# First chunk of a head without its zero-state products, and per-token columns by transposes

## The chip, the cores and the metric

The kernel runs on one core of one Trainium2 chip. The metric is device time in microseconds, from the start to the end of one execution. All matrices live in memory as fp32; most products run as three fp32r products of a high and a low part.

## What is computed

One layer of a streaming encoder, for a new stream of 2048 tokens (the prompt) and 64 tokens of a running stream (the sample), model width 1024. Cut to what matters here:

```python
h = rmsnorm(x, norm1_w)
proj = h @ w_in                 # q,k,v (4 heads x 128 each), z, a, b (4 each), pooling input
qkv = silu(causal_conv4(qkv));  q, k l2-normalised
g = -exp(a_log) * softplus(a + dt_bias);  beta = sigmoid(b)
G = cumsum(g) within a chunk    # per token and head
# per chunk and head, with state S (128 x 128):
v_new = u - w @ S               # u = T (beta v),  w = T (beta exp(G) k)
o     = (q exp(G)) @ S + (q k^T * gamma) @ v_new
S     = S * exp(G_last) + (k exp(G_last - G))^T @ v_new
x = x + concat(rmsnorm(o) * silu(z), pool(u_pool)) @ w_out
x = x + (silu(rmsnorm(x) @ w_gate) * (rmsnorm(x) @ w_up)) @ w_down
```

The prompt's state S starts at zero; the sample's comes as an input. Outputs are the tokens and the states after the last token.

## The kernel before

The work has two phases. In phase one the tokens go through in four blocks: block 0 has 512 prompt tokens and the 64 of the sample, the others 512 each. A block's normed input is multiplied by 21 weight tiles of `w_in` (names `pp`, `project`): tile 0 gives the columns a and b, then come q, k, v and z of each of four heads, then four pooling tiles. Phase two is the feed-forward part, with Strassen-like products, and isn't touched.

All instructions are first noted and then put in order by a list scheduler written in the kernel (`Machine`, its `issue`): it keeps a planned time for each engine and for each tile's buffers, and takes on each engine the operation with the lowest rank of those ready. Rank is the place in the program, less a boost: `HOT_ROWS` for the function `rows`, 400 for evictions. A tile gets a buffer of its tag when its first operation is ready. For each tag but the three common matmul banks (`psmm`, tag `mm`) only the head of the queue is looked at, so a tag's tiles get buffers in the order in which the program made them. `issue` starts all engines from that order; each engine runs its list in order.

PSUM has eight banks here: three of tag `mm`, one each of `k` and `o`, and three of tags `b0` to `b2`, given by `bank(i, name)`, each with one buffer. The chains of a head (`Front`) use `b0` to `b2` in turn; before any head is ready these banks serve the start of block 0:

```python
pab = project(B, 0)            # block 0: its halves go to banks o and k
rows(B, pab)
...                            # then head_project -> project(B, 1 + 4*h + i)
out = [[bank(("ok", (1, 2))[m][i], f"pp{m}_{i}") if B.j == 0 and m < 2 else psmm(...)
```

So in block 0 the first half of tile 1 (`pp1_0`, tokens 0 to 287) goes to bank 1 and the second half (`pp1_1`) to bank 2. Within a half, block 0 runs 24 products for each tile (8 parts of the depth times 3); in the other blocks the tokens are not halved.

A weight tile arrives as two raw parts (`wrp` in the profile), each is cast (ScalarE) and its rest subtracted (VectorE) into a split part (`wsp`, four buffers, so two tiles' worth), and in block 0 the split part is also stored to memory (`wnd<-wsp`) for the later blocks. A split part's buffer is free when its products are done and its store has landed.

`rows` makes the per-token rows from a and b: it adds the norm's factor, takes softplus, multiplies by the coefficient (`Rt`, rows 0 to 3 g, rows 32 to 35 the log of beta), sums g within each chunk of 128 tokens, and puts G_last - G in rows 64 to 67. Then it turns them into per-token columns with a product with a 0/1 matrix `sel12` for each chunk (12 columns, tile `pc`), and takes the exponential into `EC`; for the sample, the same into `ECs`. In block 0 `pc` lies in bank 0, behind two sums of the norm and one small product.

`Head.prompt` runs the recurrence over a head's four chunks of 128 tokens: product of k with S, subtraction (`rhs`), product with the inverse `X`, scaling (`vn`), state update product, and the two products of the output `po`. The state `Sp` is zeroed at the start.

Of the kernel before, what the change touches and what calls it, by code (L numbers as in the profile page):

```python
# [11 lines left out]
F32 = mybir.dt.float32  # L12
F32R = mybir.dt.float32r
AF = mybir.ActivationFunctionType
ALU = mybir.AluOpType
# [3 lines left out]
P = 128  # L19
# [5 lines left out]
C = 128  # L25
# [12 lines left out]
SO = PB[0] + 3  # L38
# [331 lines left out]
def hybrid_kernel(ctx, tc, a, o):  # L370
    nc = machine = Machine(tc.nc)
    act = nc.scalar.activation
    tt = nc.vector.tensor_tensor
    ts = nc.vector.tensor_scalar
# [7 lines left out]
    def mm(out, lhsT, rhs, start, stop, **kw):  # L382
        nc.tensor.matmul(out, lhsT, rhs, start=start, stop=stop, **kw)
        n = 1
        for d in out.shape[1:]:
            n *= d
        cost(n, rhs.dtype)
# [527 lines left out]
    B = Block(0)  # L915
# [13 lines left out]
    pcnt = names["pcnt"].rearrange("p (g t) -> p g t", t=16)  # L929
    poolw = names["poolw"].rearrange("p (g t) -> p g t", t=P)  # L930
    sgn, dtb, alog = names["sgn"], names["dtb"][:64], names["alog"][:64]
    sel12 = names["sel12"]
    hist = names["sconv"].rearrange("p (m i t) -> p m i t", i=2, t=3)
    phist = names["spool"].rearrange("p (m i t) -> p m i t", i=2, t=HP)
    Ss = names["sdelta"].rearrange("p (h v) -> p h v", v=P)
# [32 lines left out]
        nc.gpsimd.tensor_copy(*((t, x) if keep else (x, t)))  # L968

    Sp = cp1.tile([P, NH, P], F32, tag="Sp", name="Sp")  # L970
    nc.vector.memset(Sp, 0.0)

    def bc(t, nch, n):
        return t.unsqueeze(1).to_broadcast([t.shape[0], nch, n])
# [164 lines left out]
    class Head:  # L1139
# [37 lines left out]
        def prompt(self):  # L1177
            tag, h, B = self.tag, self.h, self.B
            S = Sp[:, h, :]
            po = bank("o", f"po_{tag}")  # L1180
            qsq = self.squares(512)
            for f in self.f:
                yield lambda: f.done
                for c in range(2):
                    pk = bank("k", f"pk{c}_{f.tag}")
                    mm(pk[:, :P], f.chunk(1, c), S, start=True, stop=True)
                    rhs = gp.tile([P, P], F32, tag="rhs", name=f"rhs{c}_{f.tag}", bufs=2)
                    stt(rhs, pk[:, :P], f.e(0)[:, c : c + 1], f.vtk[:, c, :], ALU.mult, ALU.subtract)
                    yield LAT_D
                    mm(pk[:, P : 2 * P], f.X[:, c], rhs, start=True, stop=True)  # L1190
                    vn = gp.tile([P, P], F32, tag="vn", name=f"vn{c}_{f.tag}", bufs=2)
                    act(vn, pk[:, P : 2 * P], AF.Copy, scale=f.kn[:, 2, c : c + 1])
                    yield LAT_D
                    osl = slice((f.c0 + c) * C, (f.c0 + c + 1) * C)
                    mm(pk[:, 2 * P : 3 * P], f.ktl[:, c, :], vn, start=True, stop=True)
                    mm(po[:, osl], S, f.Qd[:, c, :], start=True, stop=False)
                    mm(po[:, osl], vn, f.QKG[:, c], start=False, stop=True)
                    stt(S, S, f.EL[:, c], pk[:, 2 * P : 3 * P], ALU.mult, ALU.add)
                    yield LAT_D
                f.used = True  # L1200
            osq = yield from self.norm(512, po, qsq)
            if B.kept:
                nc.sync.dma_start(out=od[h], in_=osq)
                return
            yield lambda: B.o is not None
            split(B.o[h], slice(0, 512), osq)
# [36 lines left out]
    def rows(B, pab):  # L1243

        j, YW, nch = B.j, B.YW, B.nch
        Ghl = B.Ghl = gp.tile([P, SO + P], F32R, tag="Ghl", name=f"Ghl{j}", bufs=2)
        EC = B.EC = gp.tile([P, 4, 16], F32, tag="EC", name=f"EC{j}", bufs=2)
        xr = gp.tile([64, YX], F32, tag="w2", name=f"xr{j}", bufs=2)
        er = gp.tile([64, YX], F32, tag="w2", name=f"er{j}", bufs=2)
        if B.dec:  # L1250
            nc.gpsimd.memset(xr, 0.0)
        for i, b, n, dst in B.segs:
            x, lo = xr[:, dst : dst + n], B.subs[i][0] + b
            act(x, pab[i][:64, b : b + n], AF.Identity, scale=sgn[:64], bias=0.0 if j == 0 else dtb)
            stt(x, pab[i][64:, b : b + n], sgn[64:], x, ALU.mult, ALU.add)
            if j == 0:
                tt(x, x, B.r[:64, lo : lo + n], ALU.mult)
                ts(x, x, dtb, None, ALU.add)
        act(er[:, :YW], xr[:, :YW], AF.Abs)
        act(er[:, :YW], er[:, :YW], AF.Exp, scale=-1.0)  # L1260
        act(er[:, :YW], er[:, :YW], AF.Ln, bias=onec[:64])
        stt(er[:, :YW], xr[:, :YW], 0.0, er[:, :YW], ALU.max, ALU.add)
        Rt = gp.tile([P, SO + P], F32, tag="w2", name=f"Rt{j}", bufs=2)
        nc.gpsimd.memset(Rt[64:], 0.0)
        nc.gpsimd.memset(Ghl[64:].bitcast(F32), 0.0)
        ts(Rt[:64, :YW], er[:, :YW], coef, None, ALU.mult)
        chunks = [(c * C, C) for c in range(nch)] + ([(SO, DEC)] if B.dec else [])
        for lo, n in chunks:
            nc.vector.tensor_tensor_scan(Rt[0:4, lo : lo + n], ones[0:4, :n], Rt[0:4, lo : lo + n], 0.0,
                                         ALU.mult, ALU.add)  # L1270
        for c, (lo, n) in enumerate(chunks):
            ts(Rt[64:68, lo : lo + n], Rt[0:4, lo : lo + n], Rt[0:4, lo + n - 1 : lo + n], -1.0,
               ALU.subtract, ALU.mult)
        if B.dec:
            nc.vector.tensor_copy(Rt[:, SO + DEC : SO + P], Rt[:, SO : SO + DEC])
            chunks[-1] = (SO, P)
        pc = psg(f"pc{j}") if j else bank(0, "pc0")
        for c, (lo, n) in enumerate(chunks):
            mm(pc[:n, c * 12 : c * 12 + 12], Rt[:, lo : lo + n], sel12, start=True, stop=True)
        pc3 = pc[:, : 12 * nch].rearrange("p (c t) -> p c t", t=12)  # L1280
        act(EC[:, :nch, :12], pc3, AF.Exp)
        act(EC[:, :nch, 12:], pc3[:, :, :4], AF.Copy, scale=-1.0)
        if B.dec:

            ECs = B.ECs = cp1.tile([P, 4, 2], F32, tag="ECs", name="ECs")
            for i in range(2):
                t = slice(i * DEC, (i + 1) * DEC)
                of = pc[t, 12 * nch : 12 * nch + 12].rearrange("p (t c i) -> p t c i", t=3, i=2)[:, :, :, i]
                act(ECs[t, :3], of, AF.Exp)
                act(ECs[t, 3], of[:, 0], AF.Copy, scale=-1.0)  # L1290
            YW += DEC
        nc.vector.tensor_copy(Ghl[0:32, :YW], Rt[0:32, :YW])
        tt(Ghl[32:64, :YW], Rt[0:32, :YW], Ghl[0:32, :YW].bitcast(F32), ALU.subtract)
# [467 lines left out]
    for op in order:  # L1761
# [23 lines left out]
        else:  # L1785
# [56 lines left out]
WAIT_STAT = 8.46  # L1842

CONSTS = (("ident", 128), ("convw", 48), ("onw", 1), ("psc", 4), ("pcnt", 64), ("poolw", 512), ("sgn", 1),
          ("dtb", 1), ("alog", 1), ("sel12", 12), ("sel", 4), ("sconv", 72), ("spool", 120), ("sdelta", 512))


def _layout(inp):
# [56 lines left out]
        lm[:, l, :] /= WSCALE  # L1905
    lm[:, 7, :] = np.where(i[None] >= i[:, None], 0.0, -1e30)
    r["lmask"] = lm
    z = np.zeros((P, 12), f32)
    for t in range(3):
        for h in range(4):  # L1910
            z[32 * t + h, 4 * t + h] = 1.0
    c["sel12"] = z
    z = np.zeros((P, 4), f32)
    for h in range(4):
        z[h, h] = 1.0
# [40 lines left out]
```

## Time and profile before

| | before |
|---|---|
| median of three runs | 2296.41 us |
| lowest and highest run | 2295.73, 2298.98 us |
| span of the profiled execution | 2295.8 us |
| TensorE busy | 2271.8 us (99%) |
| VectorE busy | 1711.3 us (75%) |
| ScalarE busy | 1342.1 us (58%) |
| GpSimd busy | 833.4 us (36%) |

The span goes from the first to the last instruction of one profiled execution; the page gives no other time of that execution, and the median of the runs is 0.6 us above it. In the profile PE is TensorE and PEld its weight loads, DVE VectorE, ACT ScalarE, POOL GpSimd, SPq the queue of SyncE that issues DMAs. Every instruction has line 285, the helper that issues the planned order, so work is told apart by its tiles: `out<-in`. An fp32 product is two records of TensorE, an fp32r product or a transpose one. A row of the timeline gives its start, the time from its first to its last end, engine, operation, tiles, count, and in brackets an idle time before it with what ended it. A row by tile gives count, shortest, median and longest duration in ns, and the first and last start.

### The profile page before, as it was taken

What the parts mean: (1) busy time and instruction counts of PE and PEld (TensorE: products, weight loads), DVE (VectorE), ACT (ScalarE), POOL (GpSimd) and SP (SyncE); (2) the same over time, 40 slices, a digit from 0 to 9 for tenths busy, and PEclk for the clock granted to TensorE, in tenths of its full rate; (3) what the DMA queues carried; (4) which work ended last, traced back from release to release, by engine and by line L of the source; (5) the groups of instructions that cost most, each with busy time, mean ns of one, the idle gap of its engine ahead of it and who ended that gap; (6) DMA issues with size and microseconds to landing.
All of it is one profiled execution on the core that took longest, in us unless ns stands there. A gap on an engine that the chain in (4) does not pass through costs nothing.

```text
span 2295.8 us, 41549 instructions
## 1 busy us (share of the span) xinstructions
PE 2271.8 (99%) x14518; PEld 2132.1 (93%) x14518; DVE 1711.3 (75%) x3129; ACT 1342.1 (58%) x3039; POOL 833.4 (36%) x893
## 2 busy tenths in 40 slices
PE   8999999999999999999999999999999999999998
PEld 8898898888787888999999999999999999999998
DVE  8989876685678896788888786866667768666576
ACT  6986866684769864565446366554334574353344
POOL 3425342453247450565434236622111453010112
PEclk9999999999999999999999999999999999999999
DMA  8755586578476767866776578778765776666653
GB/s 295 263 182 193 199 294 234 191 238 277 159 245 232 212 212 254 304 247 247 272 260 238 185 264 292 248 266 302 234 198 199 263 271 230 209 216 224 210 195 103
DMA packets 256514, 536.96 MB, mean 234 GB/s; under 512 B 30000, under 2 KB 94000, under 8 KB 256304
## 3 DMA queue, kind: packets, MB, share of 16 engines
q1 hardware_dynamic: 255728, 533.58, 69.3%
q8 instruction: 114, 1.87, 0.3%
q14 instruction: 96, 0.79, 0.1%
q10 hardware_dynamic: 576, 0.72, 0.1%
HBM read 403.62 MB, written 130.58 MB: 233 GB/s over the span
## 4 chain that ended last, share of the span: by engine, by line
PE 88%; DVE 5%; DMA 3%; ACT 2%; issue 1%; POOL 1%; SPq 0%; DVEq 0%; POOLq 0%; ACTq 0%
PE px L285 21%; PE pp L285 17%; PE pz L285 13%; PE py L285 10%; PE dx L285 8%; PE dy L285 4%; PE d L285 3%; PE dz L285 2%; PE pk_p L285 2%; PE pt_p L285 2%; PE gr_p L285 1%; DVE y L285 1%; PE py_p L285 1%; DVE h L285 1%; DMA hpd<-xt 1%
## 5 line engine op out<-in xcount | busy, mean ns | idle before, releaser
L285 PE MATMUL pp<-h,wsp 128*128 128x512 f32 (+1 forms) x2480 | 547.9, 364 | 10.0 <-DVE wsp L285 10.0
L285 PEld LDWEIGHTS pp<-h,wsp 128*128 128x128 f32 x2480 | 401.4, 189 | 58.2 <-ACT wsp L285 9.2
L285 ACT CAST ws<-wr 128x512 fp32r<-128x512 f32 x198 | 122.1, 618 | 166.7 <-PE dx L285 55.2
L285 DVE TENSOR_TENSOR ws<-wr,ws 128x512 fp32r<-128x512 f32 x198 | 173.4, 879 | 30.9 <-ACT ws L285 27.1
L285 POOL TENSOR_TENSOR q<-hr,hr 128x352 f32<-128x352 f32 x52 | 58.0, 1116 | 369.6 <-DVE hr L285 366.8
L285 ACT CAST wsd<-wrd 128x512 fp32r<-128x512 f32 (+1 forms) x120 | 62.6, 526 | 174.8 <-PE dx L285 66.8
L285 DVE TENSOR_TENSOR y<-y,dx 128x352 f32<-128x352 f32 x240 | 121.8, 517 | 57.0 <-PE dx L285 56.0
L285 PE MATMUL pz<-op,wsp 128*128 128x288 f32 (+1 forms) x768 | 163.0, 353 | 0.0
L285 PE MATMUL px<-hA,ws 128*128 128x352 f32 x792 | 145.2, 322 | 0.0
L285 ACT ACTIVATE hr<-g 128x352 f32<-128x352 f32 x132 | 65.6, 497 | 133.7 <-DVE g L285 133.5
L285 PE MATMUL py<-hA,wsS 128*128 128x352 f32 x792 | 141.5, 322 | 2.0 <-DMA wsS<-gS 1.6
L285 PE MATMUL py<-hB,wsS 128*128 128x352 f32 x792 | 141.7, 322 | 0.0
L285 PE MATMUL pz<-hB,ws 128*128 128x352 f32 x792 | 141.0, 322 | 0.0
L285 ACT CAST TV_p<-pt_p 128x512 f16<-128x512 f32 x192 | 110.4, 589 | 49.6 <-PE pt_p L285 49.2
L285 PE MATMUL px<-hA,wsS 128*128 128x352 f32 x792 | 138.5, 322 | 0.0
L285 PE MATMUL px<-hBT,wsS 128*128 128x352 f32 x792 | 137.9, 322 | 0.2 <-ACT g L285 0.2
L285 PE MATMUL px<-hBT,ws 128*128 128x352 f32 x792 | 137.7, 322 | 0.0
L285 PEld LDWEIGHTS pz<-op,wsp 128*128 128x128 f32 x768 | 120.9, 188 | 12.1
L285 PEld LDWEIGHTS py<-hA,wsS 128*128 128x128 f32 x792 | 129.4, 188 | 2.6 <-DMA wsS<-gS 1.9
L285 PEld LDWEIGHTS px<-hA,ws 128*128 128x128 f32 x792 | 130.0, 188 | 0.1
L285 PE MATMUL dy<-hq,wsdS 128*128 128x352 f32 x672 | 129.6, 322 | 0.0
L285 PEld LDWEIGHTS py<-hB,wsS 128*128 128x128 f32 x792 | 129.4, 188 | 0.0
(697 smaller groups left out, 5777.2 us busy)
## 6 DMA issues: line engine op xcount, KB each, us to landing
wsS<-gS SPq DMA_DIRECT2D x176, 512.0 KB, 4.5
wsp<-wnd SPq DMA_DIRECT2D x126, 512.0 KB, 3.8
gS<-wsS SPq DMA_DIRECT2D x88, 512.0 KB, 4.9
wsdS<-dsd SPq DMA_DIRECT2D x88, 512.0 KB, 4.4
wr<-in_wg_dram SPq DMA_DIRECT2D x132, 256.0 KB, 3.5
wnd<-wsp SPq DMA_DIRECT2D x42, 512.0 KB, 5.0
wrd<-in_wd_dram SPq DMA_DIRECT2D x68, 256.0 KB, 2.7
xd<-x2d SPq DMA_DIRECT2D x96, 176.0 KB, 4.1
```

Source lines behind the costliest of these rows:

```text
L285: getattr(getattr(self.nc, op.eng), name)(*args, **kw)
```

## The change

For the first chunk of the prompt in block 0, each head leaves out the product with the zero state, the subtraction, the product of S with the query, and the update of S: X is applied to v itself, the scaling (now on VectorE) has the other sign, and S is a copy (on ScalarE) of the update product. The state isn't zeroed any more. In `rows`, the 12-column products with `sel12` become transposes of the 128 x 128 pieces of `Rt` against the identity, and the exponential reads its 12 columns a chunk out of 128. The sample's columns get a tile of their own, `pcs`, in bank 1. `sel12` goes from the constants.

```diff
-    sel12 = names["sel12"]
...
     Sp = cp1.tile([P, NH, P], F32, tag="Sp", name="Sp")
-    nc.vector.memset(Sp, 0.0)
...
                 for c in range(2):
                     pk = bank("k", f"pk{c}_{f.tag}")
-                    mm(pk[:, :P], f.chunk(1, c), S, start=True, stop=True)
-                    rhs = gp.tile([P, P], F32, tag="rhs", name=f"rhs{c}_{f.tag}", bufs=2)
-                    stt(rhs, pk[:, :P], f.e(0)[:, c : c + 1], f.vtk[:, c, :], ALU.mult, ALU.subtract)
-                    yield LAT_D
-                    mm(pk[:, P : 2 * P], f.X[:, c], rhs, start=True, stop=True)
+                    begin = B.dec and f.c0 + c == 0
                     vn = gp.tile([P, P], F32, tag="vn", name=f"vn{c}_{f.tag}", bufs=2)
-                    act(vn, pk[:, P : 2 * P], AF.Copy, scale=f.kn[:, 2, c : c + 1])
+                    if begin:
+                        mm(pk[:, P : 2 * P], f.X[:, c], f.vtk[:, c, :], start=True, stop=True)
+                        ts(vn, pk[:, P : 2 * P], f.kn[:, 1, c : c + 1], 1.0 / WSCALE, ALU.mult, ALU.mult)
+                    else:
+                        mm(pk[:, :P], f.chunk(1, c), S, start=True, stop=True)
+                        rhs = gp.tile([P, P], F32, tag="rhs", name=f"rhs{c}_{f.tag}", bufs=2)
+                        stt(rhs, pk[:, :P], f.e(0)[:, c : c + 1], f.vtk[:, c, :], ALU.mult, ALU.subtract)
+                        yield LAT_D
+                        mm(pk[:, P : 2 * P], f.X[:, c], rhs, start=True, stop=True)
+                        act(vn, pk[:, P : 2 * P], AF.Copy, scale=f.kn[:, 2, c : c + 1])
...
                     mm(pk[:, 2 * P : 3 * P], f.ktl[:, c, :], vn, start=True, stop=True)
-                    mm(po[:, osl], S, f.Qd[:, c, :], start=True, stop=False)
-                    mm(po[:, osl], vn, f.QKG[:, c], start=False, stop=True)
-                    stt(S, S, f.EL[:, c], pk[:, 2 * P : 3 * P], ALU.mult, ALU.add)
+                    if begin:
+                        nc.scalar.copy(S, pk[:, 2 * P : 3 * P])
+                    else:
+                        mm(po[:, osl], S, f.Qd[:, c, :], start=True, stop=False)
+                    mm(po[:, osl], vn, f.QKG[:, c], start=begin, stop=True)
+                    if not begin:
+                        stt(S, S, f.EL[:, c], pk[:, 2 * P : 3 * P], ALU.mult, ALU.add)
...
         if B.dec:
             nc.vector.tensor_copy(Rt[:, SO + DEC : SO + P], Rt[:, SO : SO + DEC])
-            chunks[-1] = (SO, P)
         pc = psg(f"pc{j}") if j else bank(0, "pc0")
-        for c, (lo, n) in enumerate(chunks):
-            mm(pc[:n, c * 12 : c * 12 + 12], Rt[:, lo : lo + n], sel12, start=True, stop=True)
-        pc3 = pc[:, : 12 * nch].rearrange("p (c t) -> p c t", t=12)
-        act(EC[:, :nch, :12], pc3, AF.Exp)
-        act(EC[:, :nch, 12:], pc3[:, :, :4], AF.Copy, scale=-1.0)
+        for c in range(nch):
+            transpose(pc[:, c * P : (c + 1) * P], Rt[:, c * C : (c + 1) * C], ident)
+        pc3 = pc.rearrange("p (c t n) -> p c t n", c=nch, t=4)
+        act(EC[:, :, :12].rearrange("p c (t h) -> p c t h", h=4), pc3[:, :, :3, :4], AF.Exp)
+        act(EC[:, :, 12:], pc3[:, :, 0, :4], AF.Copy, scale=-1.0)
         if B.dec:
             ECs = B.ECs = cp1.tile([P, 4, 2], F32, tag="ECs", name="ECs")
+            pcs = bank(1, "pcs")
+            transpose(pcs[:, :P], Rt[:, SO : SO + P], ident)
             for i in range(2):
                 t = slice(i * DEC, (i + 1) * DEC)
-                of = pc[t, 12 * nch : 12 * nch + 12].rearrange("p (t c i) -> p t c i", t=3, i=2)[:, :, :, i]
+                of = pcs[t, :96].rearrange("p (t n) -> p t n", t=3)[:, :, i:4:2]
                 act(ECs[t, :3], of, AF.Exp)
                 act(ECs[t, 3], of[:, 0], AF.Copy, scale=-1.0)
```

More of the change, by code (lines that the diff above doesn't have):

```diff
@@ L1844 @@
 CONSTS = (("ident", 128), ("convw", 48), ("onw", 1), ("psc", 4), ("pcnt", 64), ("poolw", 512), ("sgn", 1),
-          ("dtb", 1), ("alog", 1), ("sel12", 12), ("sel", 4), ("sconv", 72), ("spool", 120), ("sdelta", 512))
+          ("dtb", 1), ("alog", 1), ("sel", 4), ("sconv", 72), ("spool", 120), ("sdelta", 512))
 def _layout(inp):
@@ L1907, in _layout @@
     r["lmask"] = lm
[L1908 to L1912, printed above, removed]
     z = np.zeros((P, 4), f32)
```

## The prediction

> **What bounds the kernel now.** I read the page first: the busy times and the chain that ended last.
>
> ```profile
> span 2295.8 us, 41549 instructions
> PE 2271.8 (99%) x14518; PEld 2132.1 (93%) x14518; DVE 1711.3 (75%) x3129; ACT 1342.1 (58%) x3039; POOL 833.4 (36%) x893
> PE 88%; DVE 5%; DMA 3%; ACT 2%; issue 1%; POOL 1%; SPq 0%; DVEq 0%; POOLq 0%; ACTq 0%
> ```
>
> TensorE is busy for 99% of the span and makes 88% of the chain. So a TensorE slot that is saved is saved in the total, and a hole that is torn into TensorE's work is paid in full: only some 24 us of idle exist to absorb it, 9.2 of them before the first product. Next I read the busy time by stretches for the place that the change touches, the first block:
>
> ```profile
> 9.20:23.00 13.80, 13.02 (x83) 12.79 (x83) 12.83 (x28) 11.18 (x29) 5.86 (x7) 1.00 1.03 393
> 23.00:30.00 7.00, 7.00 (x52) 6.84 (x53) 5.80 (x11) 5.27 (x13) 5.44 (x6) 1.00 0.81 281
> 30.00:46.50 16.50, 16.18 (x125) 15.87 (x124) 14.21 (x37) 9.52 (x23) 5.59 (x12) 1.00 0.79 285
> 46.50:58.00 11.50, 11.50 (x89) 11.50 (x88) 11.35 (x21) 7.92 (x16) 1.80 (x4) 1.00 0.69 235
> 58.00:110.00 52.00, 51.71 (x413) 47.29 (x412) 48.06 (x94) 47.60 (x123) 25.64 (x31) 1.00 0.73 253
> ```
>
> After the length come TensorE, weight loads, VectorE, ScalarE, GpSimd. TensorE has no room from 23 us on; VectorE is nearly as full. What fills TensorE between 9 and 58 us is one stream of projections (pp), told apart in the timeline of TensorE alone:
>
> ```profile
> 9.19 12.95 PE L285 MATMUL pp<-h,wsp 128*128 128x288 f32 x82 [9.19 <-DVE wsp L285]
> 22.92 1.98 PE L285 MATMUL pp<-h,wsp 128*128 128x288 f32 x13 [0.78 <-DVE wsp L285]
> 24.87 0.95 PE L285 MATMUL pp<-h,wsp 128*128 128x288 f32 x6
> 25.98 6.65 PE L285 MATMUL pp<-h,wsp 128*128 128x288 f32 x49
> 33.20 0.95 PE L285 MATMUL pp<-h,wsp 128*128 128x288 f32 x6
> 34.12 4.01 PE L285 MATMUL pp<-h,wsp 128*128 128x288 f32 x29
> 38.01 5.42 PE L285 MATMUL pp<-h,wsp 128*128 128x288 f32 x39
> 44.08 1.43 PE L285 MATMUL pp<-h,wsp 128*128 128x288 f32 x9
> 45.48 12.85 PE L285 MATMUL pp<-h,wsp 128*128 128x288 f32 x95
> ```
>
> By the code, block 0's row projection (weight tile 0) has 32 products and every later tile 48: 24 for each half of the tokens. So the 82 products up to 22.1 us are tiles 0 and 1 and two of tile 2. The last row gives the price of one, 12.85/95, less the tail of the last: 0.133 us.
>
> **The change, part by part. (a) The products with the zero state.** Per head, K·S and S·Qd of the first chunk go, 8 fp32 products of 128 columns. Each is two records. In this piece of the full timeline the weight loads of one K·S product start at 58.49 and the next ones at 58.71:
>
> ```profile
> 58.03 0.49 PEld L285 LDWEIGHTS ptk_p<-consts,Yqk 128*128 128x128 f32 x4
> 58.49 0.30 PEld L285 LDWEIGHTS pk_p<-Sp,Yqk 128*128 128x128 f32 x2
> 58.71 0.30 PEld L285 LDWEIGHTS fp<-fw,consts 128*128 128x128 f32 x2
> ```
>
> That is 0.22 us a product, 1.8 us for eight; they lie in a full TensorE, so all of it counts. On VectorE two operations a head go and one comes; on ScalarE a copy comes for a scaling. None of these is shown; the nearest rows are the scaling out of PSUM that goes and the state update that goes:
>
> ```profile
> L285 ACT ACTIVATE vn_p<-pk_p,kn_p x64: 342/368/424, 115.2 to 875.9; 128x128 f32<-128x128 f32 x64
> L285 DVE SCALAR_TENSOR_TENSOR Sp<-Sp,EL_p,pk_p x64: 331/340/350, 117.3 to 877.4; 128x128 f32<-128x128 f32 x64
> ```
>
> At 0.34 to 0.37 us each they change VectorE by minus 0.34 us a head and ScalarE by about nothing, beside projections that keep TensorE busy: taken at 0, bounds minus 0.4 us (if VectorE is the limit) and plus 0.4. The zeroing of the state lies before any VectorE work that waits, and the constants' load is only 6 KB shorter (128 x 12 words): 0.
>
> **(b) Transposes for selection products.** 16 products of a prompt chunk and one of the sample, each with 12 columns, become 17 fp32 transposes. The rows:
>
> ```profile
> 43.14 0.99 PEld L285 LDWEIGHTS pc<-consts,Rt 128*128 128x128 f32 x8
> 44.05 1.22 PEld L285 LDWEIGHTS pp<-h,wsp 128*128 128x128 f32 x9
> ...
> L285 PE MATMUL ptk_p<-consts,Yqk x64: 270/273/328, 58.2 to 808.5; 128*128 128x128 f32 x64
> ```
>
> Eight records (four products) hold the weight path from 43.14 to 44.05: 0.23 us each. A transpose of the same size is the ptk row of (a): four from 58.03 to 58.49, 0.115 us each. 17 x 0.115 = 2.0 us saved, in all four blocks. The readings of the result into EC keep their element counts (48 and 16 a chunk set): 0. Gain of (a) and (b): 3.8 us, with the bounds of (a)'s side engines 3.4 to 4.2. The Trainium skill (TensorE: Matmul & The Clock Gate, Part 4: PE-mode transpose) gives about 275 ns for a transpose in a kernel; the trace's record of one is as long (270 to 328 ns), but four start within 0.46 us, so the start distance decides. If 275 ns were the price in the stream, (b) would cost 0.8 us (an estimate from that page) in place of saving 2.0.
>
> **(c) The bank.** This is the term that decides the sign. The sample's columns now go to a tile of bank 1, made inside `rows`. Bank 1 has one buffer, and the order by hand serves such a tag strictly first come first served. `rows(B, pab)` runs before `head_project`, whose first projection puts its first half (pp1_0) into `bank(1)`. So pp1_0 now stands behind the whole chain of the rows, which ends late, with the last reading of ECs:
>
> ```profile
> 35.33 0.38 DVE L285 TENSOR_TENSOR xr<-xr,rn 64x224 f32<-64x224 f32 x1 [1.11 <-ACT rn L285]
> 44.36 0.19 DVE L285 COPY Rt<-Rt 128x64 f32<-128x64 f32 x1
> 45.84 0.46 ACT L285 ACTIVATE ECs<-pc 64x6 f32<-64x6 f32 x4
> ```
>
> That chain depends on the norm and not on pp1_0, so I leave it in place: bank 1 comes free at about 45.9 instead of before 16 us. TensorE does not stop for all that time: pp1_1 has bank 2, and later tiles have three other banks. But pp1_0 keeps both halves of weight tile 1 occupied, and the split weights (wsp) have four buffers, two for a tile. From tile 3 on each tile has to wait for the buffers of the one before it, which need their store to memory landed. Those steps are in the timelines of ScalarE, VectorE and the SP queue, as they are now for tiles 2 and 4 (tile 4 takes tile 2's buffers):
>
> ```profile
> 21.57 2.50 DVE L285 TENSOR_TENSOR wsp<-wrp,wsp 128x512 fp32r<-128x512 f32 x2
> 25.73 0.82 SPq L285 DMA_DIRECT2D wnd<-wsp  x1
> 28.94 0.60 ACT L285 CAST wsp<-wrp 128x512 fp32r<-128x512 f32 x1
> 29.57 1.31 DVE L285 TENSOR_TENSOR wsp<-wrp,wsp 128x512 fp32r<-128x512 f32 x1
> 31.07 0.62 ACT L285 CAST wsp<-wrp 128x512 fp32r<-128x512 f32 x1 [1.52 <-DMA wnd<-wsp]
> 33.41 0.90 SPq L285 DMA_DIRECT2D wnd<-wsp  x2
> 39.47 0.62 ACT L285 CAST wsp<-wrp 128x512 fp32r<-128x512 f32 x1
> 46.97 0.68 DVE L285 TENSOR_TENSOR wsp<-wrp,wsp 128x512 fp32r<-128x512 f32 x1
> ```
>
> Walking through it: tile 1 starts at 15.7 now (48 x 0.133 before 22.1), so pp1_1 runs from 15.7 to 18.9, and TensorE then idles until the first half of tile 2 is split, 22.8 (half of the 2.50 from 21.57). Tile 2 ends at 29.6, as now. Tile 3 gets tile 2's buffers, at the times tile 4 has now: ready at 30.9 (29.57 + 1.31), second half by 33. It ends at 37.9 (48 products and about 0.6 of norm products). Its stores go out where tile 4's go now, 33.41; a store issued at 25.73 released the cast of 31.07, 5.3 us later, so tile 4's cast can start at 38.7 and its split is done at 40.2 (0.62 + 0.68 and a short queue). From 40.2 to 45.9, less 0.7 of transposes, 37 products run. By 45.9 the new kernel has 32 + 24 + 48 + 48 + 37 = 189 projection products behind it; now it is 233 up to 45.45 (the sum of the rows above but the last) and 3 more: 236. The lag is 47 x 0.133 = 6.3 us. Afterwards pp1_0 itself covers the next split, tile 1's buffers come free, and the stream is as before. The late q of the first head delays its SiLU by some 7 us, but its fronts, which start at 58 us, then lag no more than TensorE itself: nothing added. The lag isn't regained, for the reason given at the start.
> Bounds of (c): tile 4 without a gap (T = 37.9) leaves a lag of 3.9 us (29 products); its subtraction pushed behind the rows work on VectorE, as the one at 46.97 is now (its cast was at 39.47), to 43.6, makes 9.6 us (72 products).
>
> Sum against the profiled execution: 2295.8 + 6.3 - 3.8 = 2298.3. The median of the runs lies 0.6 us over that span, so 2298.9 on the runs' scale, 0.1% over 2296.41. This kernel's times can tell about 0.2%, 4.6 us, from no change: 2291.8 to 2301.0 counts as the same.
>
> **The rivals.** *VectorE order (other side, slower).* Place: the subtraction of tile 4's first half, at 39 to 44 us. The rows' operations carry a priority over it; now one such subtraction waits from 40.1 to 46.97. If it slips past 42.4 the lag passes 8.4 us and the net 4.6; at 43.6 it is 9.6, net +5.8: 2302.2. Against it: tile 4 is noted before the first head's convolution and so ranks ahead of that, which the one at 46.97 does not.
>
> *Clock.* The first products after a long idle run slowly: the weight loads of the stream's first microsecond against those five microseconds later, and the granted clock after the last product:
>
> ```profile
> L285 PEld LDWEIGHTS pp<-h,wsp x4: 285/330/333, 9.2 to 9.8; 128*128 128x128 f32 x4
> L285 PEld LDWEIGHTS pp<-h,wsp x9: 187/187/188, 13.9 to 15.0; 128*128 128x128 f32 x9
> 2290.00:2291.00 1.00, 0.00 (x0) 0.00 (x0) 1.00 (x3) 0.00 (x0) 1.00 (x2) 0.50 0.70 254
> ```
>
> The slow loads last from 9.2 to about 13 us, half speed for 3.9 us, a loss of at most 1.9. A gap of 3.9 us (18.9 to 22.8) could bring that back; the loss would vanish in the wait for tile 3 (29.6 to 30.9) and mostly in that for tile 4. Only if the gap before tile 4 (2.3 us) halves the clock as well does 1.9 us stay: net +4.4, 2300.8. By the Trainium skill (TensorE: Matmul & The Clock Gate, Part 1) an idle window of about 3.4 us sends the clock to half; by that rule the first gap does it and the second not. The trace agrees as far as it goes: the gap of 0.78 us at 22.1 brought no slow loads.
>
> *Full stop.* If the buffers were bound in turn, tile 3 would wait for tile 1's buffers, and TensorE would stand from 29.6 to 45.9: 236 - 104 = 132 products, 17.6 us, net +13.8: 2310.2. Against it: the order written by hand gives whichever buffer is free.
>
> *The wait is hidden.* If the rows end early, by some 8 us, or the order finds room, the lag falls to 3.2 (the 24 products of the first gap) or less, and the gain of 3.8 leaves 2295.8 or lower, down to 2292.6 without any lag, or 2292.2 with (a)'s upper bound. For it: TensorE's stretch is full of other work; against it: the chain's rows above start only with the norm at 35.33.
>
> **How the numbers follow.** Forecast, lag 3.9 to 8.4: 0.50. VectorE order: 0.20. Clock: 0.08. Full stop: 0.06. Hidden: 0.16, of which half without any lag. The hidden case without lag ends at 2292.6, 0.8 us short of a measurable gain, so faster gets most of that half, for gains that I have not seen, 0.07; slower takes VectorE order, full stop and the half of the clock case that meets a larger lag, with some of the forecast's upper edge, 0.34; the same is 0.59. From 2293 to 2306 leaves out the full stop, the best of the hidden case, and little else. The forecast's own range is 2296 to 2301.
>
> **What would show it.** Right: pp's first stretch shrinks from 82 to about 56 products and is followed by an idle of some 4 us that ends with wsp; more waits of pp for wsp at 30 and 38 to 40 us; 24 pp right after ECs near 46; projections of the first block about 6 us later at 58 us; pc with 16 and pcs with one transpose of single records; K·S (pk with Sp) 8 records fewer. Wrong: no idle before 22 us (the bank isn't shared as I read it), or one idle up to 46 us (full stop); weight loads of 330 ns at 23 or 40 us (clock); a lag that shrinks again in later blocks (TensorE was not the limit there).

## The result and the profile after

The changed kernel takes 2307.39 us (median of 4 runs, 2304.1 to 2308.9). Against four runs of the kernel before (median 2296.80) the ratio is 1.0041, 95% interval 1.003 to 1.0053. Below, a ratio is also turned into microseconds, as its distance from one times 2298, which is near the medians of the kernel before in all rounds: here 9.4 us slower (6.9 to 12.2). The two medians lie 10.6 us apart, inside that interval. The forecast was 2.5 us slower, in a range from 2293 to 2306.

The head of the page of after:

```profile
span 2306.1 us, 41505 instructions
PE 2271.1 (98%) x14485; PEld 2130.2 (92%) x14485; DVE 1699.5 (74%) x3124; ACT 1344.0 (58%) x3039; POOL 827.9 (36%) x893
```

TensorE's row is busy for as long as before (2271.1 to 2271.8 us), although it holds 33 records fewer, and the span is 10.3 us longer. TensorE's timeline of after, up to 47 us (start, length, operation, count, and in brackets the idle time before it and what ended it):

```profile
9.42 9.99 PE L285 MATMUL pp<-h,wsp 128*128 128x288 f32 x56 [9.42 <-DVE wsp L285]
20.44 0.79 PE L285 MATMUL pp<-h,wsp 128*128 128x288 f32 x4 [1.03 <-ACT wsp L285]
23.08 2.64 PE L285 MATMUL pp<-h,wsp 128*128 128x288 f32 x18 [1.84 <-DVE wsp L285]
...
30.72 1.46 PE L285 MATMUL pp<-h,wsp 128*128 128x288 f32 x9 [0.41 <-DVE wsp L285]
...
38.77 0.80 PE L285 MATMUL pp<-h,wsp 128*128 128x288 f32 x4 [1.30 <-ACT wsp L285]
40.55 1.98 PE L285 MATMUL pp<-h,wsp 128*128 128x288 f32 x13 [0.98 <-DVE wsp L285]
...
43.80 1.46 PE L285 MATMUL pp<-h,wsp 128*128 128x288 f32 x9 [0.29 <-DVE wsp L285]
45.09 0.27 PE L285 MATMUL pcs<-consts,Rt 128*128 128x128 f32 x1
...
45.92 1.48 PE L285 MATMUL pp<-h,wsp 128*128 128x288 f32 x9
```

The first stretch is 56 products, not 82; then TensorE waits for split weights at 20.4, 23.1, 30.7, 38.8 and 40.6; and the stream runs on at 45.92, once ECs has read `pcs`. The weight loader's list of waits from 46 us on shows this last wait (total, times, longest in us):

```profile
PEld pp L285 <- ACT ECs L285: 0.5, 1, 0.5
```

That is the course that part (c) walked through, but for four products at 20.44, which needed only the cast half of their weights. How many projection products lie behind each kernel by 45.9 us is one row of the busy time by stretches, for the tile `pp` alone (length, TensorE's busy time and count), first of before, then of after:

```profile
9.20:45.90 36.70, 34.55 (x236) 1.00 0.90 329
```

```profile
9.20:45.90 36.70, 29.18 (x180) 1.00 0.79 281
```

56 products at 0.133 us are 7.4 us of lag (forecast: 47, 6.3). But that is not all. The first feed-forward products show how late phase one ends, the last ones what is left at the end:

```profile
L285 PE MATMUL px<-hA,ws x792: 317/322/326, 933.0 to 2241.6; 128*128 128x352 f32 x198
```

```profile
L285 PE MATMUL px<-hA,ws x792: 317/323/326, 946.8 to 2251.9; 128*128 128x352 f32 x198
```

Phase one ends 13.8 us later, so some 6 us more were lost behind the first 46 us, and the 3.8 us of savings are not to be seen; phase two gives 3.5 back. In the busy time by stretches, TensorE alone, the idle time (length less busy) has grown in the later blocks too, where the change touches nothing but the four transposes of a block, first before, then after:

```profile
425.00:640.00 215.00, 215.00 (x1308) 1.00 0.66 222
640.00:850.00 210.00, 209.50 (x1362) 1.00 0.73 229
```

```profile
425.00:640.00 215.00, 212.13 (x1278) 0.99 0.67 219
640.00:850.00 210.00, 206.84 (x1334) 1.00 0.71 222
```

### The profile page after: what moved, and what is told of

It reads as the page before. It is cut to its first block, busy times and chain, and to the rows that moved or that the text cites. A ratio compares the mean times of both kernels' runs of the same rounds, so it can differ in the third digit from the quotient of the medians.

```text
span 2306.1 us, 41505 instructions
## 1 busy us (share of the span) xinstructions
PE 2271.1 (98%) x14485; PEld 2130.2 (92%) x14485; DVE 1699.5 (74%) x3124; ACT 1344.0 (58%) x3039; POOL 827.9 (36%) x893
## 4 chain that ended last, share of the span: by engine, by line
PE 87%; DVE 5%; ACT 3%; DMA 2%; issue 1%; POOL 1%; SPq 0%; DVEq 0%; ACTq 0%; POOLq 0%
PE px L285 21%; PE pp L285 16%; PE pz L285 12%; PE py L285 11%; PE dx L285 9%; PE dy L285 4%; PE d L285 3%; PE dz L285 2%; PE pk_p L285 2%; PE pt_p L285 1%; PE gr_p L285 1%; DVE y L285 1%; PE py_p L285 1%; ACT E L285 1%; DMA xd<-x2d 1%
## 5 line engine op out<-in xcount | busy, mean ns | idle before, releaser
L285 DVE TENSOR_TENSOR ws<-wr,ws 128x512 fp32r<-128x512 f32 x198 | 170.3, 863 | 30.7 <-ACT ws L285 26.8
```

The source lines that it names most:

```text
L285: getattr(getattr(self.nc, op.eng), name)(*args, **kw)
```

## The experiments

Three theories, as the expectations name them. Theory 1: the bank costs its 7 us, and the later waits follow from that lag. Theory 2: the early lag is the bank's, but the later waits come from the order, which the scheduler makes anew for any changed list of operations. Theory 3: the new operations cost more than they save.

### The bank and the two parts, each in an order made anew

**The whole change without bank 1.** `pcs` goes to bank 0, behind `pc0`:

```
-            pcs = bank(1, "pcs")
+            pcs = bank(0, "pcs")
```

> The whole change, but the sample's columns go to bank 0 behind pc0 instead of bank 1. Theory 1 (the bank costs its lag of 7 us at the start, and the waits on TensorE in the later blocks follow from that lag): the gap of TensorE at 19 to 23 us and those at 30 to 44 us go, and the later waits with them; time 2293 (2296.8 less the 3.8 that the removed work saves). Theory 2 (the early lag is the bank's, but the later waits come from any newly planned order, whatever the cause): the gaps before 46 us go, the idle of TensorE between 58 and 900 us stays in the range of 2 to 10 us; time 2294 to 2302. Theory 3 (the new operations themselves cost more than they save): 2300 or more with no early gap.

2300.6 us, ratio 1.0007 (0.9999 to 1.0016), 1.6 us over before. TensorE's busy row of the first stretch is that of before again (35.69 there):

```profile
9.20:46.00 36.80, 35.77 (x250) 1.00 0.90 328
```

**The bank alone.** The kernel before; only the sample's selection product goes to a tile of its own in bank 1:

```
-        for c, (lo, n) in enumerate(chunks):
+        for c, (lo, n) in enumerate(chunks[:nch]):
...
+            pcs = bank(1, "pcs")
+            mm(pcs[:, :12], Rt[:, SO : SO + P], sel12, start=True, stop=True)
```

> The kernel before, with nothing but the sample's selection product moved to a tile of its own in bank 1. Theory 1: the early gaps as in the changed kernel and the later waits too, 2307.4 plus the 3.8 not saved: 2309 to 2312. Theory 2: the early gaps (+7) and a later part of its own, 2301 to 2311, with the later waits at other places than in the changed kernel. Theory 3: as before, 2296.8.

2310.34 us, ratio 1.0048 (1.0035 to 1.006), 11 us slower. The bank is the large term: 7.8 us between after and the kernel with bank 0 (9.4 less 1.6, each with some 2 to 3 us to either side). In this trace TensorE's clock fell, in the gap that the bank tears (the number behind the count is the granted clock):

```profile
21.00:22.00 1.00, 0.00 (x0) 0.89 1.05 430
22.00:23.00 1.00, 0.81 (x3) 0.50 0.76 311
...
26.00:27.00 1.00, 1.00 (x10) 1.00 1.05 430
```

Its price was gone at the wait for tile 3, which ends at 30.76 us here and at 30.72 in the changed kernel, whose clock did not fall there; by 45.9 us 181 projection products were done, against 180.

**Part (a) alone**, nothing of (b):

```
+                    begin = B.dec and f.c0 + c == 0
...
+                    if begin:
+                        nc.scalar.copy(S, pk[:, 2 * P : 3 * P])
+                    else:
+                        mm(po[:, osl], S, f.Qd[:, c, :], start=True, stop=False)
```

> Only the first chunk without the zero-state products; the columns as before. Theory 1: 2296.8 less 1.8: 2295. Theory 2: the pk products fall by 8 records and the early stretch is as before, but the time is 2294 to 2301 by where new waits fall. Theory 3: slower than 2297 with the later blocks unchanged in their waits.

2300.27 us, ratio 1.0006 (0.9997 to 1.0015).

**Part (b) alone**, with the sample's transpose in bank 0:

```
+            transpose(pc[:, c * P : (c + 1) * P], Rt[:, c * C : (c + 1) * C], ident)
...
+            pcs = bank(0, "pcs")
```

> Only the transposes for the selection products, the sample's in bank 0; the first chunk as before. Theory 1: 2296.8 less 2.0: 2294.8. Theory 2: the pc group takes half its time in the weight path, but the time is 2293 to 2301 by where new waits fall. Theory 3: slower than 2297, with the chain of the rows longer in each block.

2303.47 us, ratio 1.0016 (1.0007 to 1.0025). Neither part gains. Theory 1 falls: without the bank, TensorE still idles over 2 us in 640 to 850 us in each of these kernels (2.8, 2.4, 3.4). Theories 2 and 3 are left.

### The same parts with the order held

Here every operation is noted, ranked and laid out just as before, and only when a finished order is issued is the operation replaced or dropped, so that each engine runs the rest in the order of before. The helper is two lines, and `issue` skips an operation without a call:

```
+    def instead(call):
+        machine.ops[-1].call = call
...
                     mm(po[:, osl], S, f.Qd[:, c, :], start=True, stop=False)
+                    if begin:
+                        instead(None)
```

**Part (a), held.** The products go; the subtraction becomes a negation of v, and the scaling and the update of S stay as they were, so that only TensorE has less to do:

> Part (a) alone, with the order held: every operation is laid out with the operations and durations of the kernel before, and only then are the 8 fp32 products of the first chunk dropped (and VectorE's and ScalarE's operations put in their new form). Every engine issues what is left in the order of the kernel before. Theory 2 (the savings are real, and what eats them in the re-planned kernels is the other order that the planner makes of the changed list): the 8 products of 0.22 us come out, 1.8 us under the kernel before, and TensorE's idle of 640 to 850 us, which was 2.4 us where the order was planned anew, stays at the 0.5 us of before. Theory 3 (the dropped slots were hidden or the new operations cost what they save): 0, the same as before within 0.5 us. Theory 1 says nothing here, since the bank is not touched: minus 1.8 as well.

2296.53 us, ratio 0.999 (0.9982 to 0.9999), 2.3 us faster. **Part (b), held** (transposes of 96 rows, all five of block 0 in the one bank):

> Part (b) alone with the order held as in the run of part (a): the 17 selection products become transposes (of 96 rows, so that all five of a block fit into the one bank that is used before), each in the place of its product. No new bank. Theory 2: 17 x 0.115 us saved, 2.0 us under the kernel before; idle of 215 to 425 and 640 to 850 us as before (0.46 and 0.5 us, against 4.56 and 3.44 where the order was planned anew). Theory 3: the transposes cost more than they save, so 0 to 4 us over the kernel before, with the waits of pc for Rt (2.3 us in the re-planned kernel) still there.

2296.59 us, ratio 0.9992 (0.9983 to 1.0001), 1.8 us faster. That leaves Theory 3 little room for each part alone: by the ratios they save about what they were priced at, though the intervals reach from some 4 us down to nothing. Single traces do not show that saving at the end of phase one, where `px` starts at 933.5 and 932.5 us, against 933.0 before. What they show is the price being paid out, and taken back. TensorE around the first dropped product, before:

```profile
58.16 0.60 PE L285 MATMUL ptk_p<-consts,Yqk 128*128 128x128 f32 x4
58.60 0.39 PE L285 MATMUL pk_p<-Sp,Yqk 128*128 128x128 f32 x2
58.82 1.02 PE L285 MATMUL fp<-fw,consts 128*128 128x512 f32 x2
...
60.92 0.39 PE L285 MATMUL gb_p<-Ghl,selp 128*128 128x256 f32 x1 [0.28 <-ACT ktl_p L285]
```

and with part (a) held:

```profile
58.02 0.60 PE L285 MATMUL ptk_p<-consts,Yqk 128*128 128x128 f32 x4
58.45 1.02 PE L285 MATMUL fp<-fw,consts 128*128 128x512 f32 x2
...
60.78 0.38 PE L285 MATMUL gb_p<-Ghl,selp 128*128 128x256 f32 x1 [0.52 <-ACT ktl_p L285]
```

The lead grows from 0.14 to 0.37 us with the product that is gone: 0.23, its price. Two microseconds on, `gb_p` needs ScalarE's `ktl_p`, waits 0.52 instead of 0.28, and the lead is 0.14 again. The transposes likewise: in the kernel before the four products hold TensorE from 43.27 to 44.08, with (b) held from 42.88 to 43.18:

```profile
43.27 0.95 PE L285 MATMUL pc<-consts,Rt 128*128 128x12 f32 x8
44.08 1.43 PE L285 MATMUL pp<-h,wsp 128*128 128x288 f32 x9
```

```profile
42.88 0.52 PE L285 MATMUL pc<-consts,Rt 96*128 96x96 f32 x4
43.18 1.43 PE L285 MATMUL pp<-h,wsp 128*128 128x288 f32 x9
```

0.13 us saved for each (priced 0.115), and part of that too goes at the next meetings: in the last block the wait of `os_p` for VectorE's `lo_p` near 680 us is 0.47 us instead of 0.24.

**How much of a TensorE slot counts.** The four products S.Qd of the first chunks are too few to measure that, so all 64 of the prompt are dropped, and in a second kernel made twice, the order held in both:

```
                     mm(po[:, osl], S, f.Qd[:, c, :], start=True, stop=False)
+                    instead([])
...
                     mm(po[:, osl], vn, f.QKG[:, c], start=False, stop=True)
+                    instead(("matmul", (po[:, osl], vn, f.QKG[:, c]), dict(start=True, stop=True)))
```

```
                     mm(po[:, osl], S, f.Qd[:, c, :], start=True, stop=False)
+                    instead([("matmul", (po[:, osl], S, f.Qd[:, c, :]), dict(start=True, stop=x)) for x in (True, False)])
```

> The kernel before with its order held and all 64 products S.Qd of the prompt chunks dropped, not just the four of the first chunks (the part of the output that comes from the state is left out). Each is 0.22 us on TensorE; no other engine's work changes. If TensorE alone is the bound, as the prediction had it: 64 x 0.22 = 14.1 us faster. If the side engines' chain of a head has so little slack that TensorE waits for it at the next meeting (in the trace of the first-chunk products alone each dropped product moved TensorE 0.22 us ahead and most of that was given back at the next wait for ktl_p or X_p): a fraction, 2 to 6 us faster, and TensorE's idle of 46 to 930 us, 1.9 us before, grows by 8 to 12.

> The counterpart: the order held and each of the 64 products S.Qd of the prompt chunks made twice (the second overwrites the first, so nothing is left out). 64 x 0.22 = 14.1 us are added to TensorE. If TensorE alone is the bound: 14.1 us slower, as much as the kernel with 64 products fewer is faster. If TensorE and the side engines are tied with little slack on either side: near the full 14 us slower (10 to 14, some of it falling into waits that TensorE has anyway), though the kernel with fewer products gains only a fraction. If those products lie in holes: under 5.

Dropped: 2291.74 us, ratio 0.9969 (0.9958 to 0.998), 7.1 us faster of 14.1. Twice: 2309.53 us, ratio 1.0049 (1.0037 to 1.0062), 11.3 us slower of 14.1. So about half of a slot saved counts and about four fifths of one added; both intervals reach some 2.5 to 3 us to either side. In the trace with the 64 dropped, which is of the slowest of its seven runs, phase one ends only 3.5 us sooner, and TensorE's idle of 46 to 930 us grew by 4.0, not by the 8 to 12 expected: the larger part of what was given back does not show as idle. The waits of the weight loader (PEld) in 46 to 930 us show more of it, before and with the 64 dropped (total, times, longest):

```profile
PEld gb_p L285 <- ACT ktl_p L285: 1.5, 5, 0.5
...
PEld pk_p L285 <- ACT vn_p L285: 0.6, 1, 0.6
...
PEld pk_p L285 <- DVE rhs_p L285: 0.5, 2, 0.3
```

```profile
PEld gb_p L285 <- ACT ktl_p L285: 4.5, 12, 0.6
PEld pk_p L285 <- ACT vn_p L285: 2.5, 4, 0.9
PEld pk_p L285 <- DVE rhs_p L285: 1.8, 4, 0.7
```

These are the steps of a head's chain on ScalarE and VectorE, and the three waits grew by 6.2 us. A busy share of 99% hides how close they are: an fp32 record lasts 0.27 us and starts 0.115 us after the one before it, so that a stall up to 0.16 us stays inside a "busy" TensorE (both figures in the prediction's rows). In 46 to 930 us the matmul row is busy for 882.1 of 884 us and the weight loads for 748.7. The Trainium skill says as much (Perfetto Trace Analysis, Identifying the Most-Contended Engine): matmul busy is no good measure of how close a kernel is to its limit, the weight loads' share is one. The trace agrees: that share is 85%. All this holds in an order that was planned with the products; what a slot is worth in an order planned without it was not measured.

### Orders made anew, with the work of before

Two kernels change nothing but one figure of the scheduler's program order, by which the operations get other ranks:

```
-LAT_A = 1.5
+LAT_A = 1.6
```

> The kernel before with one figure of its planner moved a little (LAT_A 1.5 to 1.6 us, the lag that the planner assumes after one kind of step), so the work is unchanged and only the order is made anew. Theory 2 (any newly made order costs what the order of before happens not to): 2 to 6 us slower than the kernel before, with idle of 2 us or more on TensorE somewhere between 200 and 900 us, where before has 0.5 in each stretch. Theory 3 (orders made anew are as good as before's, the losses come from the changed operations): within 1 us of before.

2304.64 us, ratio 1.0028 (1.0018 to 1.0038), 6.4 us slower. And with `LAT_D` from 1.5 to 1.6 instead:

> A second kernel with the work of before unchanged and the order made anew: LAT_D 1.5 to 1.6 us, the lag that the planner assumes after the products of a head's state. The first of this kind (LAT_A) took 5.9 us more than before. Theory 2 (an order made anew costs some us, whatever it was made for, because the order of before is one of the good ones): 2 to 7 us slower. If the first was a single bad draw: within 1 us of before, or faster.

2302.14 us, ratio 1.0018 (1.0009 to 1.0027), 4.1 us slower. With the three re-planned kernels above that have no new bank, five orders made anew stand 1.4 to 6.4 us over the one of before, with unchanged work and with less; two of them, at 1.4 and 1.6, are not clear of zero by their intervals. Theory 2 stands: the order of before is a good draw, and a change of the list draws again. The expected idle came with `LAT_A` (3.55 us of 215 to 425 us); with `LAT_D` no stretch of 215 to 850 us has more than 1.1, so where its 4.1 us went is not shown.

### Both parts, held, and one small store

Now both parts together, in the order of before, still without a new bank:

> Parts (a) and (b) with the order held, no new bank. Theory 2: minus 3.8 us, the sum of the prediction's (a) and (b), so about 2293 where the kernel before takes 2296.8. Theory 3: no gain, or a loss of up to 4 us as in the re-planned kernel with transposes alone.

2302.36 us, ratio 1.0012 (1.0004 to 1.0021): 2.8 us slower, where each part alone gained. The number is in Theory 3's range, but its reason, operations that cost more than they save, does not go with the gain of each part alone; neither theory fits. The lag against before is 0.7 us at 790 us, about 4 at 805 and 3.4 from 817 on. (The 0.7 says little: the kernel without the store, below, is the same program up to there, and its trace stands 0.4 us ahead of before.) In the full timeline of that place:

```profile
793.96 0.32 SPq L285 DMA_DIRECT2D xd<-x2d  x1
...
794.33 0.43 SPq L285 DMA_DIRECT2D out_cprompt_dram<-consts  x1
...
795.88 1.72 SPq L285 DMA_DIRECT2D hpd<-xt  x1
...
803.07 0.58 DVE L285 SCALAR_TENSOR_TENSOR xd<-xd,nw,r 128x352 f32<-128x352 f32 x1 [4.83 <-DMA xd<-x2d]
...
804.63 0.49 PE L285 MATMUL pk_p<-rhs_p,X_p 128*128 128x128 f32 x2 [2.76 <-DVE rhs_p L285]
```

A store of the convolution state, 18 KB in 1536 pieces of 12 bytes, is issued on the SP queue. The DMA engines are then busy and move little, and an issue on SP takes 1.72 us. The load of `xd` that VectorE needs had gone out 0.37 us ahead of the store and landed 9.0 us after its issue; VectorE stands in its order for 4.83 us until then, and `rhs_p`, which TensorE needs, is behind it on VectorE. In the kernel before the same store went out at 794.69; there too the load went out 0.37 us ahead of it, but it landed after 2.5 us, and VectorE had no wait:

```profile
794.32 0.32 SPq L285 DMA_DIRECT2D xd<-x2d  x1
...
797.46 0.58 DVE L285 SCALAR_TENSOR_TENSOR xd<-xd,nw,r 128x352 f32<-128x352 f32 x1
```

What made the difference is not shown. The transfer ahead of that load (`hpd<-xd`) had gone out 2.8 us before the small store in the kernel before and 1.7 us before it here, and was late here too: it landed 10.2 us after its issue instead of 3.7. Without the store:

```
+        late = [x for x in out if x.eng == "sync" and x.call and "cprompt" in x.call[2]["out"].tensor.name]
+        out = [x for x in out if x not in late]
```

> The kernel with parts (a) and (b) in the held order took 2302.4 us, 3.6 more than the kernel before beside it, where each part alone took 2.2 less. Its trace lags 0.7 us up to 790 us and 3.4 us from 805 us on. At 794.3 the SP queue issues one small store, out_cprompt_dram (128x12x3 values in 1536 pieces of 12 bytes); for the next 6 us the DMA engines are over 100% busy and move 20 to 170 GB/s, the next loads come late, VectorE stands 4.8 us for xd and TensorE 2.8 us for rhs_p. This kernel is the same one without that store (the output of the prompt's convolution state is left out, all else is computed). Theory S (the small store is what the lost time hangs on): TensorE's idle of 640 to 850 us falls from 4.0 to under 1.0, the time falls by 3 to 4 us to about 2299, and what is left shows what (a) and (b) are worth in sum. Theory H (the store is harmless, in the kernel before it costs nothing either; VectorE's lateness comes from the dropped products): the idle of 640 to 850 stays at 3 to 4 us and the time at 2302.

2296.53 us, ratio 0.9994 (0.9985 to 1.0002). Theory S: 4.1 us are gone between the two, and with them TensorE's idle of 640 to 850 us (4.0 to 0.5). The busy time by stretches with the store (TensorE's busy time, clock, DMA share, GB/s), and without:

```profile
796.00:802.00 6.00, 5.87 (x39) 1.00 1.15 94
802.00:808.00 6.00, 3.04 (x22) 1.00 0.89 256
```

```profile
796.00:802.00 6.00, 6.00 (x49) 1.00 0.63 181
802.00:808.00 6.00, 6.00 (x43) 1.00 0.78 271
```

With it the DMA share is 1.15 at 94 GB/s, without it 0.63 at 181. That short pieces are slow on the way to memory is also in the Trainium skill (DMA: Bandwidth & Descriptors, Why small descriptors are slow); the trace agrees, and shows that the transfers around them pay.

Two more tell whether the other kernels pay for that store too, the kernel before and the changed kernel as it is, each without it:

> The kernel before in its own order without the store out_cprompt_dram (that output is left out). Its trace has only 0.5 us of idle between 640 and 850. Theory S: in this order the store happens to cost nothing that TensorE sees, so the time is within 1.5 us of before, and the gain of 5.9 us seen with parts (a) and (b) is one of coincidence with that order's timing. Rival: the store always costs about 6 us, then 2291 to 2293.

> The changed kernel as it is, in its own newly made order, without the store out_cprompt_dram (that output is left out). Theory S: of its 3.16 us of idle in 640 to 850 us some 2 to 3 go, 2304 to 2306 where the changed kernel takes 2307.4 to 2309 beside this before; the bank's 7 us stay. Rival (that idle belongs to the order and not to the store): no change, within 1 us.

Before: 2297.48 us, ratio 0.9993 (0.9984 to 1.0002): the store costs it at most 3.7 us, most likely 1.6. After: 2306.03 us, ratio 1.0027 (1.0016 to 1.0039), 3.2 us less than with it, though the two intervals overlap; its idle in 640 to 850 us goes from 3.16 to 1.34, less than the 2 to 3 expected:

```profile
640.00:850.00 210.00, 208.66 (x1349) 1.00 0.71 224
```

The last one looks for a version that beats both kernels: both parts held, and the store moved behind a later one of its kind.

```
+        at = max(i for i, x in enumerate(out) if x.eng == "sync" and "pprompt" in ...) + 1
+        out[at:at] = late
```

> Parts (a) and (b) in the held order, nothing left out, with the small store out_cprompt_dram moved from its place near 794 us to right behind the store of out_pprompt_dram near 840 us. Theory S: the idle of 640 to 850 us goes from 4.0 to under 1, as without the store, and the stretch of 845 to 855, where VectorE has 10.0 of 10 us busy, may take a part of it back: 2296 to 2299, faster than the kernel before by up to 2 us. Theory H (it costs the same wherever it stands): 2301 to 2303.

2301.08 us, ratio 1.0007 (0.9998 to 1.0016). Theory H's number. The loss moved with the store: 794 to 808 us is free of idle, and the store, now issued at 839.66, stands before an issue on SP that lasts 3.25 us; VectorE again has a wait before its work on `xd`, of 3.49 us, and TensorE one of 2.59:

```profile
844.24 3.25 SPq L289 DMA_DIRECT2D hpd<-xt  x1
```

```profile
851.66 0.49 PE L289 MATMUL po_p__2837<-Qd_p,Sp 128*128 128x128 f32 x2 [2.59 <-DVE osq_p__2740 L289]
```

Of the kernels that leave nothing out, part (a) with the order held is the fastest: 2.3 us under before, its interval just clear of one.

## Why the prediction was wrong

Forecast +2.5 us, measured +9.4. The miss of 6.9 has two parts.

**(c), the bank, right in mechanism, 1 to 1.5 us too small.** Forecast 6.3, measured 7.4 by the count of products and 7.8 between after and the kernel with bank 0 (that pair differs in its order too, so the count is the better figure). Its steps came as walked through: 56 products in the first stretch, the waits for tiles 3 and 4 (30.7 against 30.9, 40.6 against 40.2), the stream back at 45.9. By 40.2 us 156 products had run, against 152. The mis-sized term is the last stretch: "From 40.2 to 45.9 ... 37 products run". 24 did (13, 2 and 9); the next split part came only at 43.80, after VectorE had worked on `Rt` from 40.42 to 43.05, and 9 products later TensorE's order had the product that waits for ECs, with 20 of tile 4's 48 still to come. The forecast took tile 4 for ready as a whole when its first half was. "The lag isn't regained" held, but for 3.5 us in phase two. There the kernel before had 6.1 us of idle on TensorE (935 to 2290 us) and after has 1.1, so a part of phase two did not wait for TensorE; the prediction had named a shrinking lag as a sign against it.

**(a) and (b), right in price, wrong in what counts.** Forecast -3.8, measured +1.6 in the kernel that has both and no new bank. The step that failed is the first reading, "a TensorE slot that is saved is saved in the total", drawn from 99% busy. The prices were right: 0.23 us a product, 0.13 us saved with a transpose. But with the order held about half of a saved slot goes into the next waits for ScalarE or VectorE: 14.1 us removed brought 7.1 (4.6 to 9.7). For the 3.8 us here that is a loss of some 2 us, an estimate. The rest of the 5.4 us between forecast and measurement is put down to the new order; that is argued from what other orders cost, not measured for this one.

**"The stream is as before" was the other failed step.** The change hands a new list to a scheduler that lays out the whole of phase one, so blocks 1 to 3 were laid out anew as well. The two re-planned kernels with unchanged work cost 6.4 and 4.1 us. The prediction had no rival for that, although the account of `issue` ahead of it says that the order comes from ranks over the whole list. In the changed kernel some 3 us of it hang on the one small store, if the medians of the runs with and without it are taken at their word.

**The rivals.** VectorE order: the split that it feared late at 43.6 was the second one, at 43.80, after a first one on time; its net, +5.8, came nearest, for a related reason. Clock: after's trace shows no fall in 15 to 46 us; the bank alone shows one (0.50 from 22 us), and the run of after without the store too. By the rule of the Trainium skill (TensorE: Matmul & The Clock Gate, Part 1), which the prediction weighed, an idle window of about 3.4 us does it. No idle in this gap was longer than 1.85 us, since four products ran in it; two traces show the fall all the same, one does not. Full stop and the hidden wait are out by the timeline.

**What stays open.** Both parts held, without the store, stand at 0.9994 to before, and before without the store at 0.9993: together the parts then gain nothing that can be told from zero, while each alone, with the store, gained about 2. The two intervals, some 2 us to either side each, leave room for a good half of the 3.8; a sharper figure was not measured. Why the orders made anew are all worse is told only by place (waits of 1 to 2 us for `Rt`, `X_p`, `ktl_p`, the small store), not by one cause.

## What to carry to other kernels

A TensorE that is 99% busy in the matmul row can still be tied with its partners: read the weight loader's waits, and count a slot saved amid dependent chains at about half (here 5 to 10 of 14 us, the order held) until a trace shows more. Where a scheduler orders a whole program, any edit draws a new order, which here was worth 1 to 6 us, more than the edit's own gain; hold the order to measure the edit, and change a neutral figure to see the spread. Before giving a tile a bank, look at who stands in that bank's queue: here one tile of 128 columns in the wrong bank cost twice what both savings were priced at.

## What was not expected of the hardware

An 18 KB store in pieces of 12 bytes slowed the transfers around it for some 6 us (1.15 DMA share at 94 to 118 GB/s), and single issues on the SP queue after it lasted up to 3.25 us instead of 0.4. And the clock fell after a short wait: in after, TensorE stood 2.22 us up to 546.16 us for weights that a DMA brings, and the granted clock of that stretch was 0.70:

```profile
545.00:550.00 5.00, 3.84 (x15) 0.70 0.65 231
550.00:555.00 5.00, 5.00 (x36) 0.95 0.96 278
```

Yet 1.84 us before 23.08 us left it at 1.00 in that trace, and in the trace without the small store, where the program is the same up to there, it fell to half from 23 to 26 us:

```profile
23.00:24.00 1.00, 0.89 (x4) 0.50 0.23 94
```

The records of the clock in the traces tell more. In every trace of this case the changes of the clock lie whole multiples of 3.413 us apart (in after at 14.566, 547.045 and 550.458 us, without the store at 12.523, 22.763 and 26.176), and each fall within the work lasts one such stretch. Over all traces, up to the last products, the five stretches in which TensorE was busy for at most 1.2 us were followed by half speed; of nineteen with 1.5 to 2.3 us three were. In after the gap near 23 us is split between two stretches with 2.2 and 1.7 us of work; without the store a stretch with 0.8 ends at 22.763. That would account for the fall in one trace and not in the other. It is worked out from traces alone, and no run tested it.
